# A two-sequence encoder layer on one core: part of the long sequence's products made by pairs with seven half products

## The chip, the cores and the metric

The kernel runs on one core of a Trainium2 chip. The metric is the device time of one execution in microseconds; the time given for a kernel is the median of its runs. PE is TensorE, DVE VectorE, ACT ScalarE, POOL GpSimd, SP SyncE, which issues most DMAs. Each engine works through its own instructions in the order in which they were written, and waits where an input or a buffer isn't ready.

## The reference, cut to what matters

One layer is applied to two sequences, of 512 and of 1024 tokens, with the same weights. The width is 1024.

```
u = x * (1 + scale) + shift                              # scale, shift, gate from a small condition
proj = u @ w_in                                          # segments: aq, af_f, af_b, ai, ag, rq, rk, rv, rg
q_a = silu(aq) * 128 ** -0.5                             # 8 heads of 128
logf, k = log(lb + (1 - lb) * sigmoid(fl)), (1 - lb) * sigmoid(-fl)       # fl = af_f forward, af_b backward
o_a = hgrn2(q_a, k_f, logf_f, ai) + flip(hgrn2(flip(q_a), flip(k_b), flip(logf_b), flip(ai)))
y_a = rms_norm(o_a) * a_norm_w * silu(ag)
y_r = layer_norm(retention in both directions of rope(rq), rope(rk), rv) * silu(rg)
g_a, g_r = split(sigmoid(u @ w_mg + b_mg))               # 2 x 1024 gate columns
s = (g_a * (y_a @ w_pa) + g_r * (y_r @ w_pb)) @ w_out
out = layer_norm(ALPHA * x + (1 + gate) * s) * ln_g + ln_b
```

hgrn2 is a gated linear attention: `o_t = sum over s <= t of q_t . (product of f between s and t) k_s v_s`, each of 128 columns with a decay f of its own.

## The kernel before

**Products.** All float32 products are made of F32R parts: a value is its high part plus the rest, and a product is three passes (high by low, low by high, high by high). A weight piece of 1024 x 128 comes as a raw load of 512 KB, ScalarE copies its high part (line 94), VectorE subtracts (line 103); `Stream` keeps the pieces in order of use, with four split pieces and two raw ones in flight, and `tick` splits the next one. `gemm_f` (line 310) makes 128 output columns for 512 tokens: 24 matmuls over 512 columns. `gemm_t` (line 321) makes 256 output columns for 128 tokens: 24 matmuls over 256 columns. Both give control back every six matmuls.

**Sequences and units.** The short sequence (g = 0) comes first, then the long one (g = 1), of two blocks of 512 tokens. In the long one there are eight A units, one for each head, whose two lanes are its two blocks, then four R units (retention), then the gates, then `pblock` and `oblock` (products with w_pa, w_pb and w_out, layer norm in `finish`). The spilled u, y and gates go through DRAM (`yd`, `gd`).

**An A unit.** `pre_A` makes three products for each lane: q, the forward and the backward forget logits; `evac` (lines 353 to 359) takes them out of PSUM with sigmoids, and `init_lane` (lines 340 to 346: one addition, two scalings, two multiplications on VectorE) starts a lane. `mid_A` makes values and the output gate (lines 390 to 393). `stages_A` is the chain of stages: levels 0, 1, 2, 4, 8, 16 (line 430) and 32, 64 (line 459), each of which multiplies queries and keys at one distance, takes the result with a predicated copy (439), multiplies the lanes' tiles by decays (414, and POOL's 416), and copies the next keys KM (403, 404); then four pairs of state transposes (489, 492) and state products (505, with updates 512 and 514); then for each lane the output products (542), its norm (546 to 557) and transposes of y (566 to 572).

**Order.** `interleave` writes a filler's matmuls with the stages spread among them by weights: the filler of unit i's stages is `mid` of unit i and `pre` of unit i + 1. Before the first unit of the long sequence the filler is `pre` of that unit, and the stages in it are the rest of the short sequence's `finish`. The gates of the long sequence (two blocks of 16 pieces) begin beside the last R unit and go on after it; from the fifth piece of the second block on, `load_y` issues the loads of y for the output products.

## Time and profile before

| | |
|---|---|
| runs | 2135.49, 2138.08, 2138.51 us, median 2138.08 |
| the profiled execution | span 2135.2 us |
| PE busy | 2108.5 us (99%), granted clock 0.998 |
| PEld, DVE, ACT, POOL busy | 1892.8 (89%), 1122.3 (53%), 746.7 (35%), 437.7 us (20%) |
| chain that ended last | PE 95% |
| long sequence, 738.5 us to the end: first products | 738.5 to 771.2 |
| A units | 771.2 to 1360, one each 74.1 us |
| last gates, to the output products | 1748.9 to 1946.2 for 870 matmuls of 512 columns |

Busy time is the sum of an engine's instructions; the chain is followed back from the last instruction through what released each step. An engine that is busy all the time bounds the kernel as long as its own instructions stand in the chain; where the chain leaves it, it waited, or was just about to.

### The profile page before, as it was taken

The numbers are of one execution on the slowest core, as the hardware profiler recorded it, in microseconds if no ns is written. First come the engines' busy times: TensorE is split into PE (matmuls) and PEld (weight loads), VectorE is DVE, ScalarE is ACT, GpSimd is POOL, SyncE is SP. The second block draws the span as 40 slices with busy tenths as digits, with TensorE's granted clock in tenths as the row PEclk, the third lists the DMA queues.
The fourth block names the chain that finished last, engine by engine and source line by source line (L and its number), as shares of the span: only waits on it lengthen the run. The fifth ranks groups of instructions, "written<-read, shape, count | busy, mean of one in ns | idle before, by whom it ended". The sixth has DMA issues, their size and how long they took to land.

```text
span 2135.2 us, 45792 instructions
## 1 busy us (share of the span) xinstructions
PE 2108.5 (99%) x19331; PEld 1892.8 (89%) x19331; DVE 1122.3 (53%) x2242; ACT 746.7 (35%) x1570; POOL 437.7 (20%) x668
## 2 busy tenths in 40 slices
PE   7999999999999999999999999999999999999997
PEld 5898899998888988899889889999999888889887
DVE  4856764644334965554565457353543442245657
ACT  3644553223322534444444435212121233322221
POOL 3322233321000332121121214332322100000101
PEclk9999999999999999999999999999999999999999
DMA  9322323246776421111111211212212256577752
GB/s 285 111 84 85 92 85 106 70 129 187 226 243 201 140 80 61 41 50 61 41 61 41 70 31 61 65 41 65 85 40 85 84 163 211 185 234 225 242 184 80
DMA packets 340205, 247.29 MB, mean 116 GB/s; under 512 B 9564, under 2 KB 303680, under 8 KB 338976
## 3 DMA queue, kind: packets, MB, share of 16 engines
q1 hardware_dynamic: 332112, 229.75, 34.9%
q10 hardware_dynamic: 6944, 12.59, 1.5%
q8 instruction: 152, 2.49, 0.5%
q0 software_dynamic: 944, 2.02, 0.3%
q14 instruction: 53, 0.43, 0.1%
HBM read 199.23 MB, written 45.10 MB: 114 GB/s over the span
## 4 chain that ended last, share of the span: by engine, by line
PE 95%; DMA 1%; DVE 1%; POOL 1%; issue 1%; ACT 1%; SPq 0%; POOLq 0%; DVEq 0%; ACTq 0%
PE g L310 41%; PE g L321 38%; PE l L542 2%; PE l L430 2%; PE t L505 2%; PE l L459 1%; PE l L742 1%; PE l L740 1%; PE t L677 1%; PE g L1171 1%; PE t L489 1%; PE l L1171 1%; PE t L707 1%; PE l L725 1%; PE t L1031 1%
## 5 line engine op out<-in xcount | busy, mean ns | idle before, releaser
L321 PE MATMUL g<-wh,u 128*128 128x256 f32 x3840 | 736.2, 287 | 0.0
L310 PE MATMUL g<-u,w 128*128 128x512 f32 x2736 | 671.7, 397 | 0.0
L321 PEld LDWEIGHTS g<-wh,u 128*128 128x128 f32 x3840 | 609.5, 191 | 8.9 <-issue 4.0
L310 PEld LDWEIGHTS g<-u,w 128*128 128x128 f32 x2736 | 499.7, 188 | 100.7 <-issue 1.2
L321 PE MATMUL g<-wl,u 128*128 128x256 f32 x1920 | 542.6, 283 | 0.0
L321 PEld LDWEIGHTS g<-wl,u 128*128 128x128 f32 x1920 | 367.1, 191 | 0.1
L103 DVE TENSOR_TENSOR w<-raw,w 128x1024 fp32r<-128x1024 f32 (+1 forms) x144 | 174.8, 1215 | 209.6 <-ACT w L94 209.5
L310 PE MATMUL g<-y,w 128*128 128x512 f32 x1152 | 261.8, 389 | 0.0
L310 PEld LDWEIGHTS g<-y,w 128*128 128x128 f32 x1152 | 216.1, 188 | 44.9
L414 DVE TENSOR_TENSOR X<-X,T 128x512 f32<-128x512 f32 x336 | 219.1, 698 | 22.2 <-issue 20.4
L94 ACT ACTIVATE w<-raw 128x1024 fp32r<-128x1024 f32 (+1 forms) x146 | 151.5, 1047 | 138.9 <-DMA raw<-in_w_pb 36.4
L103 DVE TENSOR_TENSOR wl<-raw,wh 128x1024 fp32r<-128x1024 f32 x98 | 122.6, 1262 | 104.2 <-ACT wh L94 104.2
L416 POOL TENSOR_TENSOR T<-T 128x512 f32<-128x512 f32 (+6 forms) x168 | 119.7, 739 | 83.6 <-DVE T L343 81.6
L94 ACT ACTIVATE wh<-raw 128x1024 fp32r<-128x1024 f32 x104 | 106.8, 1055 | 38.2 <-PE g L321 33.7
L321 PE MATMUL g<-wh,sl 128*128 128x256 f32 x384 | 109.0, 284 | 0.0
L446 POOL COPY A<-D 32x128 f32<-32x128 f32 x96 | 57.4, 598 | 248.4 <-DVE D L439 245.4
L321 PE MATMUL g<-wl,sh 128*128 128x256 f32 x384 | 107.6, 280 | 0.0
L321 PE MATMUL g<-wh,sh 128*128 128x256 f32 x384 | 107.6, 280 | 0.0
L403 ACT ACTIVATE KM<-X 128x256 f32<-128x256 f32 x120 | 51.5, 430 | 126.2 <-DVE X L414 122.5
L915 POOL TENSOR_SCALAR stat<-stat 128x1 f32<-128x1 f32 x12 | 9.2, 765 | 373.7 <-DVE stat L914 373.7
L826 ACT ACTIVATE sg<-g,vec 128x512 f32<-128x512 f32 x48 | 33.0, 687 | 127.2 <-PE g L310 127.2
L321 PEld LDWEIGHTS g<-wl,sh 128*128 128x128 f32 x384 | 73.3, 191 | 0.1
(197 smaller groups left out, 2390.7 us busy)
## 6 DMA issues: line engine op xcount, KB each, us to landing
raw<-in_w_in SPq DMA_DIRECT2D x122, 512.0 KB, 4.1
yd<-yT SPq DMA_DIRECT2D x96, 256.0 KB, 2.1
raw<-in_w_mg SPq DMA_DIRECT2D x48, 512.0 KB, 3.9
y<-yd SPq DMA_DIRECT2D x24, 1024.0 KB, 8.9
gd<-sg ACTq DMA_DIRECT2D x48, 256.0 KB, 2.7
raw<-in_w_pa SPq DMA_DIRECT2D x24, 512.0 KB, 4.7
raw<-in_w_pb SPq DMA_DIRECT2D x24, 512.0 KB, 4.0
gt<-gd SPq DMA_DIRECT2D x48, 256.0 KB, 4.7
```

Of the source, the lines that this page charges most:

```text
L94: self.nc.scalar.activation(out=hi, in_=raw, func=AF.Copy)
L103: self.lo.tensor_tensor(out=lo, in0=raw, in1=hi.bitcast(F32), op=ALU.subtract)
L310: T.matmul(ps, w[wi][:, k, :], a[ai](k), start=n == 0, stop=n == 3 * NK - 1)
L321: T.matmul(ps, a[ai](k, t0), w[wi][:, k, :], start=k == 0 and n == 0, stop=k == NK - 1 and ai == wi)
L403: S.activation(out=K4[:, :, 0, :], in_=halves(u.X[l][:, 0, :], h)[:, :, 0, :], func=AF.Copy)
L414: V.tensor_tensor(out=v, in0=v, in1=f, op=ALU.mult)
L416: G.tensor_tensor(out=T2, in0=Tv[:, :, :, 0], in1=Tv[:, :, :, 1], op=ALU.mult)
L430: T.matmul(ps[32 * i:32 * i + 32, c, :], km[:, c0:c0 + 32], qq, start=True, stop=True, tile_position=(0, 32 * i))
L446: G.tensor_copy(out=A[32 * i:32 * i + 32, :, 32 * i:32 * i + 32], in_=u.Dt[l][32 * i:32 * i + 32, :, :])
L505: T.matmul(ps[:, m, :], kt[:, m, :], u.Vt[l][:, c, :], start=True, stop=True)
L542: T.matmul(ps[:, c, :], a, b, start=i == 0, stop=i == len(mm) - 1)
L1171: T.matmul(acc[l, seg], w[wi][:, n0:n0 + 128], uh[0, 0, ai][:, k, :], start=k == 0 and n == 0, stop=k == 7 and n == 2)
```

## The change

For the long sequence, the twelve pairs of pieces in `PAIRED` (gate pieces 4 to 11, and the q and the forward forget pieces of all eight heads) are made ahead of the units. A pair is two pieces of 128 columns by two blocks of 512 tokens by 1024 of depth, seen as a 2 x 2 by 2 x 2 product of halves, and made with seven half products (line 939, 12 matmuls each) and sums, in place of eight (Winograd's form). The sums of the tokens' halves (`build_comb`, lines 903 to 915) are made once, those of the weights for each pair on GpSimd (`combine`, lines 926 to 929), the sums of the products on VectorE (lines 956 to 977). While the tokens' sums are made, gate pieces 0 to 3 run for both blocks (`FIRST`); gate pieces 12 to 15 stay at the end (`LAST`). Gates go to `gd` as before, finished q to `qd` and forget logits to `fd`, and `fetch` brings them back for each unit, so that `pre_A` of the long sequence makes only the backward product. The pool of the working tiles is closed and opened again around the pairs. The short sequence's last `finish` is written ahead of the early gates in one piece, and `load_y` begins at the first of the last four pieces. The other hunks (the pools' functions, the buffers' counts `C`: 8, `tt`: 2, `e`: 8, the releases of the pairs' raw pieces, removed comments) are left out here. Lines before and after: 310 is 358, 321 is 369, 430 is 500, 489 is 559, 505 is 575, 514 is 584, 542 is 612, 566 is 636, 340 to 346 are 388 to 394, 928 is 1114, 94 is 104.

```diff
         if j == len(self.todo) or (not self.parts and not self.open(j)):
             return False
         kind, ps = self.todo[j]
-        i = len(ps) - len(self.parts)
+        i = max(len(ps), 1) - len(self.parts)
         hi, lo = self.parts.pop(0)
-        raw = self.raws[j, i]
+        if kind in COMBINED:
+            m = COMBINED.index(kind)
+            if m == 0:
+                self.pairs[j] = self.combine(self.raws[j, 0], self.raws[j, 1])
+            raw = self.pairs[j - m][m]
+            if m == 2:
+                hi, lo = hi[:, 0:4], lo[:, 0:4]
+        else:
+            raw = self.raws[j, i]
         if kind == "k":
             raw = raw.rearrange("p k n -> p (k n)")[:, 0:768]
         self.nc.scalar.activation(out=hi, in_=raw, func=AF.Copy)
...
         [mk_unit("A", 1, i) for i in range(8)] + [mk_unit("R", 1, i) for i in range(4)],
     ]
+    EARLY = (0,1)
+    FIRST, LAST = range(4), range(12, 16)
+    PAIRED = [(None, n) for n in range(4, 12, 2)] + [(seg, h) for seg in EARLY for h in range(0, 8, 2)]
+    def order_pair(src, c0):
+        ws.add("s0", (src, c0), (src, c0 + 128))
+        for kind in COMBINED[1:]:
+            ws.add(kind)
     def order_pre(u):
         if u.kind == "A":
             for ls in u.wl:
                 h = u.lanes[ls[0]][0]
                 for seg in range(3):
-                    ws.add("f", (w_in, 1024 * seg + 128 * h))
+                    if u.g == 0 or seg not in EARLY:
+                        ws.add("f", (w_in, 1024 * seg + 128 * h))
         else:
             for ls in u.wl:
                 r = u.lanes[ls[0]][0]
...
     def pre_A(u):
         g = u.g
         prep_A(u)
+        if g:
+            fetch(u)
         for ls in u.wl:
-            for seg in range(3):
+            for seg in [seg for seg in range(3) if g == 0 or seg not in EARLY]:
                 j, w = ws.get()
                 for l in ls:
                     ps = gbank([128, 512])
                     yield from gemm_f(ps, w, u_f(g, u.lanes[l][1]))
                     evac(u, l, seg, ps)
                 ws.done(j)
+    def fetch(u):
+        for l in range(2):
+            h, b = u.lanes[l]
+            if 0 in EARLY:
+                u.X[l] = sb("X", [128, 4, 512])
+                u.q[l] = sb("q", [128, 512])
+                nc.sync.dma_start(u.q[l], qd[h, b])
+            for seg in (1, 2):
+                if seg in EARLY:
+                    ip, im = ((2, 0), (1, 3))[seg - 1]
+                    nc.sync.dma_start(u.X[l][:, ip, :], fd[seg - 1, h, b])
+        for l in range(2):
+            for seg in (1, 2):
+                if seg in EARLY:
+                    ip, im = ((2, 0), (1, 3))[seg - 1]
+                    X = u.X[l]
+                    S.activation(out=X[:, im, :], in_=X[:, ip, :], func=AF.Sigmoid, scale=-1.0)
+                    S.activation(out=X[:, ip, :], in_=X[:, ip, :], func=AF.Sigmoid)
     def mid_A(u):
         for wi, ls in enumerate(u.wl):
...
     ws.direct = gate_mm
-    def gates(g):
-        for b in range(NT[g] // 512):
-            for n in range(16):
+    def gate_evac(g, n, b, ps, t):
+        S.activation(out=t, in_=ps, func=AF.Sigmoid, bias=vec[:, 48 + n:49 + n])
+        S.dma_start(gd[g][n, :, 512 * b:512 * b + 512], t)
+    comb = {}
+    def build_comb():
+        for i in range(4):
+            comb[i] = [sb("C", [128, 4, 512], F32R, name="c") for _ in range(2)]
+        def piece(k):
+            f = {}
+            def sums():
+                for x, (b, half) in enumerate(((1, 0), (1, 1), (0, 0), (0, 1))):
+                    t = f[b, half] = sb("e", [128, 512], name="f")
+                    hi, lo = [uh[1, b, p][:, 4 * half + k, :].bitcast(F32) for p in range(2)]
+                    (V, G)[x % 2].tensor_tensor(out=t, in0=hi, in1=lo, op=ALU.add)
+            def mixes():
+                a21, a22, a11, a12 = f[1, 0], f[1, 1], f[0, 0], f[0, 1]
+                V.tensor_tensor(out=a22, in0=a21, in1=a22, op=ALU.add)
+                G.tensor_tensor(out=a21, in0=a11, in1=a21, op=ALU.subtract)
+                V.tensor_tensor(out=a11, in0=a22, in1=a11, op=ALU.subtract)
+                V.tensor_tensor(out=a12, in0=a12, in1=a11, op=ALU.subtract)
+            def parts():
+                for i, t in enumerate((f[1, 1], f[0, 0], f[1, 0], f[0, 1])):
+                    S.activation(out=comb[i][0][:, k, :], in_=t, func=AF.Copy)
+                    (V, G)[i % 2].tensor_tensor(out=comb[i][1][:, k, :], in0=t,
+                                                in1=comb[i][0][:, k, :].bitcast(F32), op=ALU.subtract)
+            return [Stage(sums), Stage(mixes), Stage(parts)]
+        return [s_ for k in range(4) for s_ in piece(k)]
+    def combine(r0, r1):
+        t12 = sb("tt", [128, 8, 128], name="t12")
+        t34 = sb("tt", [128, 8, 128], name="t34")
+        b11, b21, b12, b22 = r0[:, 0:4], r0[:, 4:8], r1[:, 0:4], r1[:, 4:8]
+        G.tensor_tensor(out=t12[:, 0:4], in0=b12, in1=b11, op=ALU.subtract)
+        G.tensor_tensor(out=t12[:, 4:8], in0=b22, in1=t12[:, 0:4], op=ALU.subtract)
+        G.tensor_tensor(out=t34[:, 0:4], in0=b22, in1=b12, op=ALU.subtract)
+        G.tensor_tensor(out=t34[:, 4:8], in0=b21, in1=t12[:, 4:8], op=ALU.subtract)
+        return r0, t12, r1[:, 4:8], t34
+    ws.combine = combine
+    def half(ps, w, k0, a, first, last):
+        n = 0
+        for k in range(4):
+            for wi, ai in ((0, 1), (1, 0), (0, 0)):
+                T.matmul(ps, w[wi][:, k0 + k, :], a[ai][:, k, :], start=first and n == 0, stop=n == 11,
+                         skip_group_check=True)
+                n += 1
+                if n % 6 == 0:
+                    yield 6 * 0.218
+    def gemm_pair(done):
+        a11, a12, a22 = [[uh[1, b, p][:, 4 * x:4 * x + 4, :] for p in range(2)] for b, x in ((0, 0), (0, 1), (1, 1))]
+        s1, s2, s3, s4 = [comb[i] for i in range(4)]
+        j0, w0 = ws.get()
+        p1 = gbank([128, 512])
+        yield from half(p1, w0, 0, a11, True, False)
+        j1, w1 = ws.get()
+        p6 = gbank([128, 512])
+        yield from half(p6, w1, 4, s2, True, True)
+        u2 = sb("e", [128, 512], name="u2")
+        S.activation(out=u2, in_=p1, func=AF.Copy)
+        yield from half(p1, w0, 4, a12, False, True)
+        ws.done(j0)
+        V.tensor_tensor(out=u2, in0=p6, in1=u2, op=ALU.add)
+        done(0, 0, p1)
+        p5 = gbank([128, 512])
+        yield from half(p5, w1, 0, s1, True, False)
+        ws.done(j1)
+        u4 = sb("e", [128, 512], name="u4")
+        V.tensor_tensor(out=u4, in0=p5, in1=u2, op=ALU.add)
+        (j2, w2), (j3, w3) = ws.get(), ws.get()
+        p7 = gbank([128, 512])
+        yield from half(p7, w3, 0, s3, True, False)
+        V.tensor_tensor(out=u4, in0=p7, in1=u4, op=ALU.add)
+        yield from half(p5, w2, 0, s4, False, True)
+        ws.done(j2)
+        c12 = sb("e", [128, 512], name="c12")
+        V.tensor_tensor(out=c12, in0=p5, in1=u2, op=ALU.add)
+        done(1, 1, u4)
+        yield from half(p7, w3, 4, a22, False, True)
+        ws.done(j3)
+        V.tensor_tensor(out=u2, in0=p7, in1=u2, op=ALU.add)
+        done(0, 1, c12)
+        done(1, 0, u2)
+    def pair_products():
+        for seg, x in PAIRED:
+            def done(b, i, what):
+                t = what if i + b else sb("e", [128, 512], name="c11")
+                if seg is None:
+                    gate_evac(1, x + i, b, what, t)
+                elif seg == 0:
+                    sg = sb("sg", [128, 512])
+                    S.activation(out=sg, in_=what, func=AF.Sigmoid)
+                    V.scalar_tensor_tensor(out=t, in0=what, scalar=qsc[:, x + i:x + i + 1], in1=sg, op0=ALU.mult,
+                                           op1=ALU.mult)
+                    S.dma_start(qd[x + i, b], t)
+                else:
+                    if i + b == 0:
+                        S.activation(out=t, in_=what, func=AF.Copy)
+                    S.dma_start(fd[seg - 1, x + i, b], t)
+            yield from gemm_pair(done)
+    def gates(g, ns=range(16), both=False):
+        nb = NT[g] // 512
+        for bs in [range(nb)] if both else [(b,) for b in range(nb)]:
+            for n in ns:
                 j, w = ws.get()
-                if b == NT[g] // 512 - 1:
-                    if n == 4:
+                if not both and bs[0] == nb - 1:
+                    if n == ns[4 if g == 0 else 0]:
                         more_y = load_y(g, 0, 0)
-                    if n >= 4 and more_y:
+                    if n >= ns[4 if g == 0 else 0] and more_y:
                         more_y.pop(0)()
-                ps = gbank([128, 512])
-                yield from gemm_f(ps, w, u_f(g, b))
-                t = sb("sg", [128, 512])
-                S.activation(out=t, in_=ps, func=AF.Sigmoid, bias=vec[:, 48 + n:49 + n])
-                S.dma_start(gd[g][n, :, 512 * b:512 * b + 512], t)
+                for b in bs:
+                    ps = gbank([128, 512])
+                    yield from gemm_f(ps, w, u_f(g, b))
+                    gate_evac(g, n, b, ps, sb("e" if both else "sg", [128, 512], name="sg"))
                 ws.done(j)
                 if rows_g:
                     gate_out(*rows_g.pop(0))
...
             yield from g_
     LEAD_IN = 2.5
-    PRE = {"A": 31.1, "R": 20.9}
+    PRE = {("A", 0): 31.1, ("R", 0): 20.9, ("A", 1): 31.1 * (3 - len(EARLY)) / 3, ("R", 1): 20.9}
     MID = {"A": 20.9, "R": 41.9}
     def run(gen):
-        for _ in gen:
-            pass
+        interleave(gen, 1.0, [], marks, ws)
+    def run_stages(stages):
+        while stages:
+            stages.pop(0).fn()
     with tc.manual_schedule():
         startup()
...
         for g in range(2):
             us = groups[g]
             if g:
-                interleave(pre(us[0]), 12.0, more, marks, ws)
+                close_pool()
+                open_pool("st")
+                interleave(gates(1, FIRST, True), 41.9, build_comb(), marks, ws)
+                interleave(pair_products(), 1.0, [], marks, ws)
+                close_pool()
+                open_pool("at1")
+                run(pre(us[0]))
             for i, u in enumerate(us):
                 st = stages_A(u) if u.kind == "A" else stages_R(u)
                 if i + 1 < len(us):
                     nx = us[i + 1]
-                    interleave(chain(mid(u), pre(nx)), MID[u.kind] + PRE[nx.kind], st, marks, ws, LEAD_IN)
+                    interleave(chain(mid(u), pre(nx)), MID[u.kind] + PRE[nx.kind, g], st, marks, ws, LEAD_IN)
                 else:
-                    interleave(chain(mid(u), gates(g)), MID[u.kind] + 60.0, st, marks, ws)
+                    fill = gates(g, LAST) if g else gates(g)
+                    interleave(chain(mid(u), fill), MID[u.kind] + (41.9 if g else 60.0), st, marks, ws)
             more = []
             nb = NT[g] // 512
             for b in range(nb):
...
                 interleave(oblock(g, b, st, g == 1 and b == nb - 1), 42.0, stages, marks, ws)
                 ws.lo = nc.vector
                 more = st["finish"]
+                if g == 0:
+                    run_stages(more)
+        close_pool()
 # ---- launch: one core; inputs and outputs as the reference has them ----
```

PE, A units: from level 2's matmuls to level 4's (line 500, both lanes), with the filler of `mid` between them; before, 24 such matmuls and more stand between two levels.

```order
L500 MATMUL l<-X,KM 32x32 x15
L369 MATMUL g<-wh,u 128x256
L369 MATMUL g<-wl,u 128x256
L369 MATMUL g<-wh,u 128x256 x2
L369 MATMUL g<-wl,u 128x256
L369 MATMUL g<-wh,u 128x256 x2
L369 MATMUL g<-wl,u 128x256
L369 MATMUL g<-wh,u 128x256 x2
L369 MATMUL g<-wl,u 128x256
L369 MATMUL g<-wh,u 128x256
L500 MATMUL l<-X,KM 32x32 [waits PE_49,Activation_49]
```

Between these two levels there are 12 matmuls over 256 columns. In the changed order 12 also stand ahead of level 1, level 16 and the first state transposes, and 24 ahead of levels 2, 8, 32 and 64.

PE, end of an A unit before: the last output product, the transposes of y of both lanes, and the next unit's products.

```order
L542 MATMUL l<-S,X 128x128
L310 MATMUL g<-u,w 128x512 x12
L566 MATMUL t<-ident,y 128x128 [waits Activation_49] x4
L310 MATMUL g<-u,w 128x512 x6
L566 MATMUL t<-ident,y 128x128 [waits Activation_49] x4
```

And after, at the same place.

```order
L612 MATMUL l<-S,X 128x128
L636 MATMUL t<-ident,y 128x128 [waits Activation_49] x4
L358 MATMUL g<-u,w 128x512 x6
L636 MATMUL t<-ident,y 128x128 [waits Activation_49] x4
L369 MATMUL g<-wh,u 128x256
```

The first lane's transposes now follow the second lane's output product at once, and six product matmuls stand ahead of the second lane's.

DVE, the same part of an A unit before: the last state updates (line 514), the two lanes' outputs by their gates (548), and the next unit's `init_lane` of lane 0 (340 to 346).

```order
L514 SCALAR_TENSOR_TENSOR S<-S,T_11181,t 128x128
L514 SCALAR_TENSOR_TENSOR S<-S,T_11166,t 128x128
L548 TENSOR_TENSOR y<-l,G 128x512
L340 TENSOR_TENSOR KM<-X 128x512
L343 TENSOR_SCALAR T_11368<-X,oml,lbm 128x512 x2
L346 TENSOR_TENSOR X<-T_11368,q 128x512 x2
L548 TENSOR_TENSOR y<-l,G 128x512
```

And after.

```order
L388 TENSOR_TENSOR KM<-X 128x512
L391 TENSOR_SCALAR T_11140<-X,oml,lbm 128x512 x2
L394 TENSOR_TENSOR X<-T_11140,q 128x512 x2
L584 SCALAR_TENSOR_TENSOR S<-S,T_11016,t 128x128
L584 SCALAR_TENSOR_TENSOR S<-S,T_11001,t 128x128
L113 TENSOR_TENSOR w<-raw,w 128x1024
L618 TENSOR_TENSOR y<-l,G 128x512 x2
```

`init_lane` of lane 0 moved from behind the first lane's output to ahead of the last state updates.

## Rows read from the trace of the kernel before

**Rows 1.** The page: busy times and the chain by engine.

```profile
PE 2108.5 (99%) x19331; PEld 1892.8 (89%) x19331; DVE 1122.3 (53%) x2242; ACT 746.7 (35%) x1570; POOL 437.7 (20%) x668
...
PE 95%; DMA 1%; DVE 1%; POOL 1%; issue 1%; ACT 1%; SPq 0%; POOLq 0%; DVEq 0%; ACTq 0%
```

**Rows 2.** The chain, 700 to 860 and 1700 to 1960 us: start, length, what.

```profile
738.50 32.66 PE g L310 x144
...
1748.94 197.22 PE g L310 x870
```

**Rows 3.** Stretches: length, busy PE, PEld, DVE, ACT, POOL, PEclk, DMA share, GB/s.

```profile
845.26:919.36 74.10, 74.10 (x913) 65.91 (x912) 40.85 (x78) 32.68 (x87) 15.61 (x26) 1.00 0.17 51
...
1289.90:1360.00 70.10, 69.88 (x1005) 67.87 (x1004) 40.50 (x83) 30.25 (x81) 25.11 (x37) 1.00 0.18 58
```

**Rows 4.** The chain of one A unit, 985 to 1067.5 us.

```profile
1014.90 0.69 PE l L430 x50
1015.59 3.06 PE g L321 x24
...
1054.40 0.44 PE t L505 x4
1054.84 1.38 PE g L310 x6
1056.22 2.45 PE l L542 x22
```

**Rows 5.** Timeline of a level, 1003 to 1010 us: start, length, engine, line, operation.

```profile
1005.76 0.89 PE L430 MATMUL l<-X,KM 128*32 128x32 f32 x64
1006.46 0.30 DVE L439 COPY_PREDICATED D<-mask,l 128x128 f32<-128x128 uint8 x1 [5.52 <-PE l L430]
...
1007.99 0.44 ACT L404 ACTIVATE KM<-X 128x256 f32<-128x256 f32 x1
...
1009.39 0.44 ACT L404 ACTIVATE KM<-X 128x256 f32<-128x256 f32 x1
```

**Rows 6.** The chain of the last A unit, 1289 to 1325 us.

```profile
1311.89 0.42 ACT KM L404
```

**Rows 7.** Timeline of VectorE, 1033 to 1065 us.

```profile
1054.88 0.61 DVE L514 SCALAR_TENSOR_TENSOR S<-S,T,t 128x128 f32<-128x128 f32 x2 [0.94 <-PE t L505]
...
1060.90 0.69 DVE L340 TENSOR_TENSOR KM<-X 128x512 f32<-128x512 f32 x1 [0.28 <-ACT X L359]
...
1062.42 1.29 DVE L346 TENSOR_TENSOR X<-T,q 128x512 f32<-128x512 f32 x2
```

**Rows 8.** The chain after the last output product, 1325 to 1362 us.

```profile
1350.44 1.43 PE g L321 x12
...
1353.73 0.94 PE t L566 x4
```

**Rows 9.** Timeline of GpSimd, then ScalarE, 742 to 760 us.

```profile
744.20 0.79 POOL L915 TENSOR_SCALAR stat<-stat 128x1 f32<-128x1 f32 x1 [11.50 <-DVE stat L914]
...
746.83 1.29 POOL L929 TENSOR_TENSOR h<-h,lb 128x512 f32<-128x512 f32 x1 [0.84 <-ACT h L928]
748.28 0.79 POOL L915 TENSOR_SCALAR stat<-stat 128x1 f32<-128x1 f32 x1 [0.15 <-DVE stat L914]
...
746.03 0.73 ACT L928 ACTIVATE h<-h,stat 128x512 f32<-128x512 f32 x1 [5.11 <-POOL stat L916]
...
754.98 1.05 ACT L94 ACTIVATE wh<-raw 128x1024 fp32r<-128x1024 f32 x1
```

**Rows 10.** Timeline of VectorE, 742 to 760 us: two like pairs of passes.

```profile
744.15 1.41 DVE L919 SCALAR_TENSOR_TENSOR h<-h,stat,lg 128x512 f32<-128x512 f32 x2
...
751.08 2.34 DVE L919 SCALAR_TENSOR_TENSOR h<-h,stat,lg 128x512 f32<-128x512 f32 x2
```

**Rows 11.** The page: loads of y.

```profile
y<-yd SPq DMA_DIRECT2D x24, 1024.0 KB, 8.9
```

**Rows 12.** The page: low parts on VectorE, busy us and mean ns.

```profile
L103 DVE TENSOR_TENSOR w<-raw,w 128x1024 fp32r<-128x1024 f32 (+1 forms) x144 | 174.8, 1215 | 209.6 <-ACT w L94 209.5
```

More of the change, by code (lines that the diff above doesn't have):

```diff
@@ L103, in flush @@
         self.lo.tensor_tensor(out=lo, in0=raw, in1=hi.bitcast(F32), op=ALU.subtract)
-        del self.raws[j, i]
+        kind = self.todo[j][0]
+        if kind in COMBINED:
+            m = COMBINED.index(kind)
+            if m == 0:
+                del self.raws[j, 0]
+            elif m == 2:
+                del self.raws[j - 2, 1]
+            elif m == 3:
+                del self.pairs[j - 3]
+            self.parts = []
+        else:
+            del self.raws[j, i]
         if not self.parts:
@@ L284, in layer @@
         else:
+            for n in FIRST:
+                ws.add("f", (w_mg, 128 * n))
+            for seg, x in PAIRED:
+                order_pair(*((w_mg, 128 * x) if seg is None else (w_in, 1024 * seg + 128 * x)))
             order_pre(us[0])
@@ L290, in layer @@
         for b in range(NT[g] // 512):
-            for n in range(16):
+            for n in LAST if g else range(16):
                 ws.add("f", (w_mg, 128 * n))
```

19 lines of the change are left out of this document (15 added, 4 removed).

## The prediction, made before the changed kernel was run

> **What bounds the kernel now.** I read the busy table first: PE is busy 2108.5 us of the 2135.2 us span and 95% of the chain that ended last lies on it, so nearly every matmul counts in full, and nothing else does until it makes PE wait [rows 1]. The per-line chain tells what a matmul costs: 870 of them over 512 columns, back to back, take 197.22 us, 0.2267 us each [rows 2]. The table by stretches then gives a pattern: the eight A units of the long sequence follow each other every 74.1 us (one of the cycles is shown), PE is busy all of it at a granted clock of 1.00, VectorE 40.8, ScalarE 32.7, GpSimd 15.6 [rows 3]. So an A unit has idle room on the other engines, but its stages form one long dependent chain, which is hidden only because PE has other products to do between two stages. The remaining views (chain and timeline inside one unit) are for the question how much of such filler each stage needs.
>
> **Part 1, the matmuls.** In the order before, 3888 matmuls run over 512 columns, after it 3744 (2736 plain and 1008 half products). 144 fewer at 0.2267 us is **-32.6 us**. That is twelve pairs times twelve matmuls: 84 in place of 96. Nothing else leaves PE. By place: the products ahead of the units lose 96 (-21.8 us), each of seven unit-to-unit cycles loses 96 (-21.8 each), the gates at the end lose 576 (-130.6), the four early gate pieces add 192 (+43.5), the pairs add 1008 (+228.5).
>
> **Part 2, the A-unit cycle with less filler.** A cycle without waits would be 74.09 - 21.76 = 52.3 us. But the chain of stages is as long as before, and the same stages now share 96 fewer filler matmuls: where a level followed its predecessor over 36, 24 or 18 pieces of filler, it now does so over 12 or 24 of 256 columns. What a level needs can be read in one place of before [rows 5]: its matmuls start at 1005.76; the predicated copy of lane 0 starts at 1006.46, its multiplications follow, ScalarE finishes that lane's new keys at 1008.43 (1007.99 + 0.44), 2.67 after the level's start; lane 1's keys follow 1.40 later, at 1009.83, 4.07 after the start. A level takes PE 0.69 and 24 filler matmuls 3.06 [rows 4], together 3.75: lane 0 finds its keys, lane 1 (which starts 0.35 later) just about finds them. This is the edge, and before shows it: in the last A unit, whose filler is 24 at every level, the chain leaves PE at a level and runs through VectorE and ScalarE's key copies [rows 6]. With 12 matmuls (half of 3.06, so 1.53) the next level is due at 2.22: lane 0 waits 0.45, and lane 1's half another 1.05, 1.5 in all at most; it is less when VectorE, which can start on lane 0 during the wait, is ahead for the following level. The changed order has 12 matmuls ahead of levels 1, 4 and 16 and of the first state transposes, 24 ahead of the others. Level 1's keys don't hang on a predicated copy; I cost it at nothing. I take 0.95 us for level 4, 1.3 for 16, 0.6 for the first transposes (0 to 1.5 each) and 0.3 for level 2, which stands over 24 but after the longer first level (0 to 0.5). What hides the remaining levels is the 24 matmuls; without them each would cost up to 1.5.
>
> Two more waits are in the second half of the unit. The **last state update**: before, it ran right after its matmuls (from 1054.88, 0.61 us) and the first output product started on time at 1056.22 [rows 4, 7]. In the changed order the next unit's start of lane 0 (one addition, two scalings, two multiplications: from 1060.90 to 1063.71, 2.81 us) stands ahead of it on VectorE, because its inputs come by DMA and no product has to be waited for. Between the third and the last state product PE has 6 matmuls (1.38 us) and the product itself (0.44); VectorE begins the 2.81 us some 0.6 after the third, so ends 3.4 after it, the update of 0.6 ends at 4.0, and PE would be there at 1.38 + 0.44 + 1.38 = 3.2. With the hand-overs I take 1.1 us (0 to 2.8). The **output transposes**: the second lane's transposes need squares on ScalarE, a power on GpSimd and a scaling on ScalarE; where before has only 12 pieces of 256 columns ahead of each lane's, they end 4.24 us after the last output product (1350.44 to 1354.68) [rows 8]. The changed order leaves 0.44 + 1.38 + 0.44 = 2.26 of work in that time: a wait of 1.98; I take 1.85 (1 to 2.2). Together 6.1 us a cycle, bounds 3 and 8.5: 58.4 instead of 74.1. Over seven cycles **+42.7 us** (21 to 60), more than all that the missing matmuls save.
>
> What stands behind a waiting PE is everything, since it works in order. The fetched logits (two 256 KB loads a lane) are issued about a unit ahead, and four sigmoids on ScalarE replace the four that read PSUM: nothing.
>
> **Part 3, start of the long sequence.** The rest of the short sequence's layer norm used to be spread under the first unit's products; now it stands in one piece ahead of the early gates on every engine. From before: GpSimd begins at 744.20; one round takes 4.08 us (744.20 to 748.28), because GpSimd's last addition of one row block comes ahead of the next block's first step [rows 9]. GpSimd's first step waits for VectorE, which has one low part of 1.22 [rows 12] ahead of it there; without that I put the start at 742.8, and four rounds' ScalarE steps end at 742.8 + 3 x 4.08 + 2.56 = 757.6. Behind them stand two weight splits (1.05 each) and only then the first gate's sigmoid (about 0.6), which frees a PSUM bank at about 760.3. PE, having three banks, has done three products at 738.5 + 3 x 5.44 = 754.8. **+5.4 us** (0 to 7).
>
> **Part 4, pairs.** A pair lasts 84 x 0.2267 = 19.0 us on PE. VectorE has in it three and a half low parts (1.22 each) and up to eight passes of 0.7, about 10; ScalarE three and a half high parts and some four copies or sigmoids, about 6; GpSimd four subtractions at 1.29 [rows 9], about 5. All fit. The tightest hand-over is the copy of the first half product out of its bank, behind a DMA issue on ScalarE; it has about half a microsecond. I take **+1 us** for the twelve (0 to 10). Rows that bear on the upper end: VectorE's pair of passes over two SBUF inputs takes 1.41 us alone and 2.34 when it meets GpSimd's addition [rows 10].
> The Trainium skill, "SBUF — State Buffer", section "Who interferes with whom", says that a VectorE instruction with two SBUF inputs and a GpSimd instruction that reads SBUF exclude each other, each for the other's whole length. The 2.34 agrees with that. By the rule every subtraction of the weight mixing can push a VectorE pass back by its length; that would be the third rival below.
>
> **Part 5, the tail.** The first loads of y for the output products (1 MB in four pieces) are issued during the last four gates instead of the fifth on. The last piece is issued about 5.4 us before the gates end, a pair of such loads needs 8.9 us to land [rows 11], and the first product reaches it about 2.7 us in: +0.8 without other traffic; I take **+1.5** (0 to 5).
>
> **Sum.** -32.6 + 42.7 + 5.4 + 1 + 1.5 = +18.0 on the profiled 2135.2. The median of the runs, 2138.08, lies 2.9 above that span; so 2138.1 + 18 = **2156 us**.
>
> **Rivals.** (a) *The cover holds.* VectorE gets ahead during each wait, so that the levels cost little, and the last state update slips ahead; 2.5 us a cycle, 17.5 in all, and 3 for the start: 2138.1 - 32.6 + 17.5 + 3 = 2126. For it: PE is idle only 0.2 us in the last A unit although its chain passes through VectorE and ScalarE [rows 3, 6]. Against: that unit has twice the filler at levels 4 and 16. With all waits hidden it would be 2105.5. (b) *A draw.* With the 7.9 us of parts 3 to 5, 3.5 us a cycle give 2138; 2.9 to 4.1 us a cycle are within 0.2%, which is about what a measurement here can tell from no change. (c) *VectorE held up by GpSimd in the pairs*, the other way up: one subtraction of 1.29 meeting the pass that frees a bank, every pair, costs 0.8 beyond its half microsecond of margin, on up to two places: 10 to 20 us more, 2166 to 2176. It decides once the bank's copy is more than 0.5 late. Against: the mixing is issued a piece ahead, mostly off that path. (d) *It does less than it says*, excluded for the count: the changed order has 3744 matmuls.
>
> **Chances.** The forecast (4.2 to 8 us a cycle, 2143 to 2170) 0.57, (c) or cycles longer still 0.13, (b) 0.13, (a) 0.17. The forecast's own range is 2143 to 2170. The range to hold 8 in 10 takes in the draw and half of (a) below and (c) above: 2124 to 2178. Slower by over 0.2% (over 2142.4): 0.70; within: 0.13; faster (under 2133.8): 0.17.
>
> **What would show it.** In the profile after: A units at a pitch of 58 to 59 us (52.3 if the cover holds, over 60 if it is worse); the chain leaving PE at levels 4 and 16 for the predicated copy, the multiplications and the key copies; VectorE's additions of the next unit's lane 0 between the last two state updates and PE idle ahead of the output product; 1.8 us ahead of the second transposes, released by ScalarE; PE idle about 5 us near the fourth early gate, released by ScalarE's sigmoid; pairs at 19 to 19.2 us. A pitch of 55 us or less would make the forecast wrong, as would pairs above 20.

## The result, and the profile after

The changed kernel takes 2176.22 us (median of four runs, 2175.91 to 2177.3) against 2137.3 for the kernel before on the same chips: 1.0184 times as long, 95% interval 1.017 to 1.0199, slower by some 39 us. The forecast was 2156: the sign was right, the size half of what came. 2176.22 lies above the forecast's own range (2143 to 2170) and inside the wide one (2124 to 2178). The profiled execution spans 2175.5 us, 40.3 more than before's 2135.2.

The page of the kernel after, against [rows 1]: busy times, and the chain by engine.

```profile
PE 2100.0 (97%) x19187; PEld 1879.1 (86%) x19187; DVE 1212.7 (56%) x2342; ACT 774.8 (36%) x1614; POOL 550.8 (25%) x736
...
PE 48%; DVE 6%; POOL 4%; issue 4%; ACT 3%; DMA 0%; ACTq 0%; DVEq 0%; POOLq 0%; SPq 0%
```

144 matmuls are gone, as counted, but PE's busy time fell by only 8.4 us in place of 32.6: some matmuls became slower, and some waits inside a row of the trace count as busy. PE's share of the chain that ended last fell from 95% to 48%. The waits of PE (in total, times, longest, us):

```profile
PE l L500 <- ACT KM L474: 14.3, 23, 0.9
PE t L636 <- ACT y L627: 8.3, 7, 1.2
PE g L939 <- POOL c L915: 7.7, 1, 7.7
PE l L612 <- DVE S L584: 7.1, 7, 1.0
PE g L358 <- ACT sg L885: 6.2, 2, 4.6
...
PE t L559 <- DVE X L484: 3.2, 7, 0.5
PE g L939 <- ACT sg L885: 2.9, 1, 2.9
...
PE g L939 <- ACT u L956: 0.7, 4, 0.2
```

Four of them are the A units' (lines 500, 559, 612, 636): three come seven times, once in each cycle, and the one at line 500 comes 23 times, some three a cycle. Three belong to the start of the long sequence: the gate's sigmoid (885) that frees a bank, and the token sums (915). Busy time in two stretches of the kernel after, from the first early gate to the end of the pairs and one A-unit cycle, to be read against [rows 3]:

```profile
core 0: us, PE busy (x) PEld busy (x) DVE busy (x) ACT busy (x) POOL busy (x), PEclk, DMA share, GB/s
739.12:1035.89 296.77, 279.16 (x1203) 227.88 (x1201) 160.96 (x182) 96.55 (x129) 113.78 (x80) 0.97 0.31 104
1106.22:1164.88 58.66, 53.93 (x817) 48.59 (x816) 37.17 (x73) 29.66 (x84) 16.36 (x26) 1.00 0.20 65
```

The first stretch holds 1200 matmuls over 512 columns, 272.0 us at 0.2267: it lost 24.7 us. The cycle is 58.66 long, where 52.33 would do: it lost 6.33, seven times. With landmarks in both traces (start of the long sequence, end of the first unit's own products, end of the eighth unit, start of the output products, end) the 40.3 us split up as 0.6 + 24.9 + 45.4 + 0.4 + 1.7 of losses, less 32.6 of matmuls. The 45.4 are the seven cycles (44.3) and 1.1 in the eighth unit.

PE's timeline in that cycle shows at which levels it waits (the rows at 1118.88, 1122.04 and 1129.42 are the second lane's halves of levels 2, 4 and 16), and the second lane's transposes, which also stretch:

```profile
1118.88 0.46 PE L500 MATMUL l<-X,KM 128*32 128x32 f32 x32 [0.31 <-ACT KM L474]
...
1122.04 0.46 PE L500 MATMUL l<-X,KM 128*32 128x32 f32 x32 [0.68 <-ACT KM L474]
...
1129.42 0.46 PE L500 MATMUL l<-X,KM 128*32 128x32 f32 x32 [0.94 <-ACT KM L474]
...
1163.68 1.21 PE L636 MATMUL t<-ident,y 128*128 128x128 f32 x4 [1.18 <-ACT y L627]
```

In the chain before, the same four transposes take 0.44 us:

```profile
1065.29 0.44 PE t L566 x4
```

Where the 24.9 went, in PE's timeline after (start, length, matmuls, and in brackets the idle time before):

```profile
739.12 16.51 PE L358 MATMUL g<-u,w 128*128 128x512 f32 x72
760.23 24.04 PE L358 MATMUL g<-u,w 128*128 128x512 f32 x96 [4.60 <-ACT sg L885]
785.89 5.78 PE L358 MATMUL g<-u,w 128*128 128x512 f32 x24 [1.62 <-ACT sg L885]
791.50 2.88 PE L939 MATMUL g<-u,w 128*128 128x512 f32 x12
797.31 3.09 PE L939 MATMUL g<-c,w 128*128 128x512 f32 x9 [2.93 <-ACT sg L885]
808.11 1.65 PE L939 MATMUL g<-c,w 128*128 128x512 f32 x3 [7.71 <-POOL c L915]
809.55 4.16 PE L939 MATMUL g<-u,w 128*128 128x512 f32 x12
813.55 8.32 PE L939 MATMUL g<-c,w 128*128 128x512 f32 x36
```

The 4.60 is the wait that was forecast. The other three, 12.3 us, are the token sums: the 2.93 and the 1.62 name ScalarE, but the sigmoid there stood behind ScalarE's copies of the sums. And the rows at and after the waits are long. The 9 matmuls at 797.31 take 3.09 us (2.0 at 0.2267), and the 96 gate matmuls 24.04 (21.8 at 0.2267, and about 0.16 for the last one's modelled end). The stretches say why:

```profile
760.20:785.90 25.70, 24.05 (x97) 19.41 (x97) 19.12 (x16) 9.15 (x14) 19.41 (x13) 0.92 0.34 109
797.30:808.10 10.80, 3.09 (x9) 1.97 (x9) 9.39 (x9) 3.79 (x6) 8.10 (x7) 0.56 0.30 97
830.00:860.00 30.00, 30.00 (x134) 24.85 (x133) 11.97 (x15) 10.71 (x14) 9.66 (x8) 1.00 0.31 102
```

Cut more finely, around the first and the last two waits:

```profile
757.70:764.40 6.70, 4.17 (x10) 3.30 (x11) 5.75 (x5) 3.17 (x5) 5.16 (x3) 0.50 0.62 216
764.50:798.50 34.00, 29.45 (x128) 23.72 (x128) 25.97 (x23) 13.35 (x21) 26.57 (x17) 1.00 0.21 71
798.70:812.20 13.50, 5.79 (x15) 4.02 (x14) 11.31 (x10) 3.73 (x6) 10.72 (x8) 0.50 0.19 59
```

The granted clock (third number from the right) is 0.92 and 0.56 in the longer stretches because it was at the lower of its two levels (0.50, that is 1.2 GHz) for a part of each, and at 1.00 otherwise. From these rows the lower clock cost about 5 us: 2.1 on the 96, 0.9 on the 9, and 2.0 on the next 15, which took 5.4 us (808.11 to 813.55) in place of 3.4. The Trainium skill, "TensorE: Matmul & The Clock Gate", section "HAM oscillation — how this bites in real kernels", says that waits between bursts of matmuls bring the clock down and that the next burst starts slow; these rows agree. The waits (16.9), the lower clock (5) and the waits for the copies in the pairs (0.7) make 22.6 of the 24.7; the rest is spread over the rows in small parts.

What held the sums up stands on VectorE and GpSimd after (VectorE's rows first, then GpSimd's of the same stretch):

```profile
760.06 3.44 DVE L903 TENSOR_TENSOR f<-u 128x512 f32<-128x512 f32 x2
...
764.55 0.68 DVE L907 TENSOR_TENSOR f<-f 128x512 f32<-128x512 f32 x1
766.65 0.69 DVE L909 TENSOR_TENSOR f<-f 128x512 f32<-128x512 f32 x1 [1.41 <-POOL f L908]
...
779.69 1.76 DVE L907 TENSOR_TENSOR f<-f 128x512 f32<-128x512 f32 x1 [3.69 <-POOL f L903]
```

```profile
759.01 3.93 POOL L903 TENSOR_TENSOR f<-u 128x512 f32<-128x512 f32 x2
765.31 1.30 POOL L908 TENSOR_TENSOR f<-f 128x512 f32<-128x512 f32 x1 [2.37 <-DVE f L907]
768.35 1.47 POOL L926 TENSOR_TENSOR t<-raw 128x512 f32<-128x512 f32 x1 [1.74 <-DMA raw<-in_w_mg]
```

Alone, such a pass takes VectorE 0.69 and GpSimd 1.30; side by side 1.72 and 1.97. The split has a second price: VectorE waits for GpSimd's part of each round, 1.41 us in the first, and 3.69 more in the second, because GpSimd had the first pair's weights to mix (from 768.35) before its part. Four such rounds, begun only after the layer norm (757.8), end at 809.7.

### The profile page after: what moved, and what is told of

Read it like the earlier page. It is cut to its first block, busy times and chain, and to the rows that moved or that the text cites. A ratio compares the mean times of both kernels' runs of the same rounds, so it can differ in the third digit from the quotient of the medians.

```text
span 2175.5 us, 45946 instructions
## 1 busy us (share of the span) xinstructions
PE 2100.0 (97%) x19187; PEld 1879.1 (86%) x19187; DVE 1212.7 (56%) x2342; ACT 774.8 (36%) x1614; POOL 550.8 (25%) x736
## 4 chain that ended last, share of the span: by engine, by line
PE 48%; DVE 6%; POOL 4%; issue 4%; ACT 3%; DMA 0%; ACTq 0%; DVEq 0%; POOLq 0%; SPq 0%
PE g L369 20%; PE g L358 12%; PE g L939 9%; DVE X L484 3%; POOL A L516 1%; PE t L575 1%; POOL T L486 1%; ACT sg L616 1%; PE t L747 1%; PE l L500 1%; PE l L812 1%; PE l L810 1%; POOL D L621 1%; PE t L559 1%; ACT y L627 1%
## 5 line engine op out<-in xcount | busy, mean ns | idle before, releaser
L358 PE MATMUL g<-u,w 128*128 128x512 f32 x1584 | 399.5, 400 | 6.2 <-ACT sg L885 6.2
L358 PEld LDWEIGHTS g<-u,w 128*128 128x128 f32 x1584 | 288.8, 189 | 64.7 <-ACT sg L885 7.1
L113 DVE TENSOR_TENSOR w<-raw,w 128x1024 fp32r<-128x1024 f32 (+2 forms) x132 | 156.3, 1185 | 154.0 <-ACT w L104 153.8
L104 ACT ACTIVATE w<-raw 128x1024 fp32r<-128x1024 f32 (+2 forms) x134 | 133.6, 1007 | 162.3 <-DMA raw<-in_w_pb 36.8
L486 POOL TENSOR_TENSOR T<-T 128x512 f32<-128x512 f32 (+6 forms) x168 | 133.2, 820 | 116.8 <-DVE T L391 114.8
L939 PE MATMUL g<-c,w 128*128 128x512 f32 x576 | 136.3, 392 | 10.6 <-POOL c L915 7.7
L939 PEld LDWEIGHTS g<-c,w 128*128 128x128 f32 x576 | 108.7, 189 | 34.3 <-POOL c L915 8.4
L939 PE MATMUL g<-u,w 128*128 128x512 f32 x432 | 103.8, 394 | 0.7 <-ACT u L956 0.7
L939 PEld LDWEIGHTS g<-u,w 128*128 128x128 f32 x432 | 81.9, 190 | 19.6 <-ACT u L956 2.4
L516 POOL COPY A<-D 32x128 f32<-32x128 f32 x96 | 51.6, 538 | 170.2 <-DVE D L509 167.2
```

What stands on the lines that cost most here:

```text
L104: self.nc.scalar.activation(out=hi, in_=raw, func=AF.Copy)
L113: self.lo.tensor_tensor(out=lo, in0=raw, in1=hi.bitcast(F32), op=ALU.subtract)
L358: T.matmul(ps, w[wi][:, k, :], a[ai](k), start=n == 0, stop=n == 3 * NK - 1)
L486: G.tensor_tensor(out=T2, in0=Tv[:, :, :, 0], in1=Tv[:, :, :, 1], op=ALU.mult)
L516: G.tensor_copy(out=A[32 * i:32 * i + 32, :, 32 * i:32 * i + 32], in_=u.Dt[l][32 * i:32 * i + 32, :, :])
L939: T.matmul(ps, w[wi][:, k0 + k, :], a[ai][:, k, :], start=first and n == 0, stop=n == 11, skip_group_check=True)
```

## The experiments

Each was timed beside the kernel before on the same chip. The first three are about the start of the long sequence, the others about the units, the pairs, or both.

**e1_comb_dve.** All token sums on VectorE.

```diff
-                    (V, G)[x % 2].tensor_tensor(out=t, in0=hi, in1=lo, op=ALU.add)
+                    V.tensor_tensor(out=t, in0=hi, in1=lo, op=ALU.add)
...
-                G.tensor_tensor(out=a21, in0=a11, in1=a21, op=ALU.subtract)
+                V.tensor_tensor(out=a21, in0=a11, in1=a21, op=ALU.subtract)
...
-                    (V, G)[i % 2].tensor_tensor(out=comb[i][1][:, k, :], in0=t,
+                    V.tensor_tensor(out=comb[i][1][:, k, :], in0=t,
```

> The changed kernel with all of the token sums (build_comb) on VectorE, none on GpSimd; the rest as it is. Theory 1 (in the changed kernel VectorE and GpSimd hold each other up: VectorE's two-input passes take 1.7 us beside GpSimd's and 0.69 alone): 12 passes of 0.69 a round, four rounds, are 33 us, with six low parts of 1.2 about 41 us from 757.7, so the sums end at about 799 in place of 809.7; from the start of the early gates to the end of the first unit's own products the loss falls from 24.9 to about 17, time about 2168. Rival 2 (it is the amount of work on VectorE, and GpSimd takes part of it off): the sums end later than 809.7, time 2176 to 2185. Rival 3 (only the layer norm ahead of them counts): no change in the waits, 2176.

Measured 2166.47 us, ratio 1.014 (1.0125 to 1.0155). The loss from the first early gate to the end of the pairs is 15.9. VectorE's timeline in this run:

```profile
757.28 2.48 DVE L903 TENSOR_TENSOR f<-u 128x512 f32<-128x512 f32 x4
...
769.36 4.67 DVE L903 TENSOR_TENSOR f<-u 128x512 f32<-128x512 f32 x4
...
794.62 3.56 DVE L915 TENSOR_TENSOR c<-f,c 128x512 fp32r<-128x512 f32 x4
798.10 1.21 DVE L113 TENSOR_TENSOR w<-t,w 128x1024 fp32r<-128x1024 f32 x1
```

Four sums take VectorE 2.48 us alone, where two of them took it 3.44 beside GpSimd. The same four take 4.67 from 769.36 on, where GpSimd mixes the first pair's weights until 772.29. One engine is done at 798.2, where the two together needed until 809.7. Theory 1 holds: the split is what slows the sums. How much of that is the longer passes and how much the waits of one engine for the other's part isn't told apart, since this edit takes both away. The Trainium skill, "SBUF — State Buffer", section "Who interferes with whom", has the two engines exclude each other in such passes. The pattern agrees; 1.72 in place of 0.69 is 1.03 more, not quite GpSimd's whole 1.30.

**e2_two_steps.** The layer norm under its own early gates, then the sums under four more.

```diff
-    FIRST, LAST = range(4), range(12, 16)
-    PAIRED = [(None, n) for n in range(4, 12, 2)] + ...
+    FIRST, SECOND, LAST = range(4), range(4, 8), range(12, 16)
+    PAIRED = [(None, n) for n in range(8, 12, 2)] + ...
...
+                interleave(gates(1, FIRST, True), 41.9, more, marks, ws)
                 close_pool()
                 open_pool("st")
-                interleave(gates(1, FIRST, True), 41.9, build_comb(), marks, ws)
+                interleave(gates(1, SECOND, True), 41.9, build_comb(), marks, ws)
...
-                if g == 0:
-                    run_stages(more)
```

> The changed kernel, with the short sequence's last layer norm spread again under early gate pieces 0 to 3, and the token sums under four further early gate pieces (4 to 7, taken out of the pairs: ten pairs in place of twelve, 24 matmuls or 5.4 us more). Theory 1 (the loss at the start comes from the layer norm in one piece, 5 to 15 us, and from sums that take 51 us where 46 are covered): no wait behind the layer norm, about 5 us behind the sums, loss at the start 24.9 down to about 7, time 2176 - 18 + 5.4 = 2163.5. Rival (the loss is in the pairs themselves, GpSimd's subtractions against VectorE): loss at the start stays above 18, time 2176 to 2181.

Measured 2163.65, ratio 1.0125 (1.0108 to 1.0142). PE runs 384 gate matmuls without a wait, in 87.23 us; one wait of 2.5 for the sums is left (with a stretch of 3.2 us at the lower clock right behind it), and the loss up to the end of the pairs is 6.3. Theory 1 holds.

**e3_no_sums.** The token sums left out.

```diff
-            comb[i] = [sb("C", [128, 4, 512], F32R, name="c") for _ in range(2)]
+            b, x = ((0, 0), (0, 1), (1, 0), (1, 1))[i]
+            comb[i] = [uh[1, b, p][:, 4 * x:4 * x + 4, :] for p in range(2)]
+        return []
```

> The changed kernel without the token sums: the pairs use the plain halves of u in their place (so q, the forward logits and half of the gates are other values), every matmul and all else as it is. Theory 1: what is left of the loss at the start is the wait behind the layer norm, about 5 us, and about 1 us of lower clock after it: 24.9 down to 6, time about 2157. Rival (the pairs are held up by GpSimd and VectorE): loss stays above 15, time above 2166.

Measured 2163.3, ratio 1.0123 (1.0108 to 1.0138). The time lies between the two, nearer to the rival's 2166 than to 2157. The trace, of an execution of 2160.98 us, speaks for theory 1: the wait behind the layer norm is there with 4.59, the others are gone, and the loss is 9.6, nearer to 6 than to 15. The stretch after that wait shows what I had put too low:

```profile
757.10:787.00 29.90, 29.90 (x121) 24.53 (x122) 4.19 (x4) 6.78 (x9) 8.66 (x6) 0.91 0.43 137
...
757.10:762.30 5.20, 5.20 (x12) 4.13 (x13) 1.04 (x1) 1.28 (x2) 0.00 (x0) 0.50 0.80 245
762.40:787.00 24.60, 24.60 (x110) 20.38 (x109) 3.14 (x3) 5.40 (x8) 8.66 (x6) 1.00 0.35 114
```

Its 120 matmuls take 29.9 us where 27.2 would do, because the first 5.2 us ran at a granted clock of 0.50: one wait of 4.6 costs 2.7 more behind it. The pairs lost about 2 in all.

**e4_early_q.** Only q and the gates in pairs, by `EARLY = (0,)`.

> The changed kernel with only q and the gates in pairs (EARLY = (0,)): the forward forget logits are made in the units again, so each A-unit cycle has 48 matmuls over 512 columns (10.9 us) more filler, and four pairs fewer are made (48 matmuls more in all, 10.9 us). Theory 1 (the 6.3 us that a cycle loses is lack of filler): about 1.5 us a cycle is left, time 2176 - 7 x 4.8 + 10.9 = 2153. Rival (the cycle loses because the fetched lane starts early on VectorE, and by the order of stages): the loss stays near 6 us a cycle, time about 2187.

Measured 2149.94, ratio 1.0063 (1.0048 to 1.0078). The cycle is 64.4 us, 1.2 over the 63.2 that its work takes. Theory 1 holds by its number: with twelve pairs the kernel is 26 us slower than with eight. The edit changes the order too, though: lane 0's start now has to wait for a product and stands behind the last state updates on VectorE again (1098.56 in this run, the last update at 1097.89), so the 1.0 us a cycle of that wait goes by order and not by filler. The waits at the levels fall from 14.3 to 2.4 us in all, and those ahead of both kinds of transposes are gone.

**e5_init_late.** The next unit's lane 0 started with lane 1.

```diff
-            if seg == 2:
-                init_lane(u, l)
+            if seg == 2 and (u.g == 0 or l == 1):
+                for i in range(2) if u.g else (l,):
+                    init_lane(u, i)
```

> The changed kernel, with the next unit's lane 0 started on VectorE together with lane 1 (after the unit's last output), in place of ahead of the last state updates. Theory 1 (PE waits 1.0 us a cycle at the first output product because those 2.8 us stand ahead of the last state updates): that wait goes, seven times 1.0, pitch 58.66 to about 57.7, time about 2169. Rival (the chain through the unit is what counts, and the wait moves on to the next level 0, which now finds both lanes late): pitch unchanged, time 2175 to 2178.

Measured 2185.62, ratio 1.0232 (1.0218 to 1.0246), 9.4 us slower than the changed kernel, more than the rival allowed. PE's waits in it:

```profile
PE l L501 <- ACT KM L475: 15.5, 26, 1.0
PE l L501 <- DVE KM L388: 8.8, 7, 2.1
...
PE l L501 <- DVE X L394: 7.3, 6, 1.2
```

The wait for the last state update (7.1) is gone, and 16.1 us of waits for the two lanes' starts came in its place. Theory 1 falls, and the rival's mechanism holds: the wait moved on to the next level 0, and grew. With so little filler neither place tried for the 2.8 us a lane was off the path.

**e6_q_spread.** Seven pairs (q, six gate pieces), the layer norm under pieces 0 and 1, the sums on VectorE under pieces 2 to 5.

```diff
-    EARLY = (0,1)
-    FIRST, LAST = range(4), range(12, 16)
+    EARLY = (0,)
+    FIRST, SECOND, LAST = range(2), range(2, 6), range(12, 16)
...
-    PAIRED = [(None, n) for n in range(4, 12, 2)] + ...
+    PAIRED = [(None, n) for n in range(6, 12, 2)] + ...
...
+                interleave(gates(1, FIRST, True), 20.9, more, marks, ws)
                 close_pool()
                 open_pool("st")
-                interleave(gates(1, FIRST, True), 41.9, build_comb(), marks, ws)
+                interleave(gates(1, SECOND, True), 41.9, build_comb(), marks, ws)
...
```

The sums' edit is that of e1, the removal of the layer norm in one piece that of e2.

> What the runs so far point to: pairs for q and six gate pieces only (seven pairs, 84 matmuls fewer than before, -19.0 us); the short sequence's last layer norm under early gate pieces 0 and 1, the token sums under pieces 2 to 5 and all on VectorE. Theory 1: cycles lose 1.2 us each (8.4), the start 2 to 3, the end 2: 2136.5 - 19.0 + 13 = about 2130, faster than before by 0.3%. Rival (a loss of 15 us at the start stays, whatever the order): 2143, slower than before.

Measured 2130.26 against 2136.51, ratio 0.9972 (0.9961 to 0.9983): faster than both kernels. The early gates (288 matmuls) and one A-unit cycle:

```profile
737.70:803.01 65.31, 65.31 (x290) 54.06 (x289) 53.44 (x78) 23.93 (x35) 18.38 (x17) 1.00 0.38 125
1088.34:1152.73 64.39, 64.10 (x864) 57.16 (x864) 38.59 (x74) 30.81 (x85) 19.02 (x26) 1.00 0.19 59
```

PE is busy throughout the first at a clock of 1.00: the early gates cost nothing any more, and the seven pairs behind them lose 1.5 us. The cycle is 64.39 long, again 1.2 over its work. Theory 1 holds.

**e7_q_spread_late.** As e6, the second lane's transposes of y carried over into the next unit's stages.

```diff
-                st = stages_A(u) if u.kind == "A" else stages_R(u)
+                st = late + (stages_A(u) if u.kind == "A" else stages_R(u))
+                late = [st.pop()] if g and u.kind == "A" else []
```

> As e6_q_spread, and the transposes of y of a unit's second lane are written a little after the next unit's first products, in place of at the unit's end, so that the norm ahead of them has time. Theory 1 (half of the 1.2 us that a cycle still loses is PE stretched over these transposes, 1.01 in place of 0.44): 0.6 us less a cycle, 4 us in all, about 2126. Rival (the next unit's levels come later by as much, or are squeezed): as e6_q_spread or slower by up to 5 us.

Measured 2143.84, ratio 1.003 (1.0018 to 1.0041): 13.6 slower than e6, more than the rival allowed. The wait for the last state update came back (7.2 in seven times), and 5.5 ahead of the state transposes. The carried stage moved the others: lane 0's start stands ahead of the last state update on VectorE again (1145.78, the update at 1148.50 in one cycle), as in the changed kernel. Theory 1 falls.

**e8_gates_only.** As e6 with `EARLY = ()`: three pairs, the units as before.

> As e6_q_spread, with pairs for six gate pieces only (three pairs, 36 matmuls fewer than before, -8.2 us): the units keep all three of their own products, the cycle its filler. Theory 1: cycle pitch 74.1 as before, the loss at the start and the end 4 to 5 us, time 2133. Rival (units lose as much without their fetched q, for another reason): pitch above 75, time above 2140.

Measured 2130.5, ratio 0.9976 (0.9967 to 0.9986); PE's waits for keys in the units are 0.5 us together, as before. Theory 1 holds for the units, and the rest lost 2 in place of 4 to 5.

**e9_plain_ahead.** As e6, its seven pairs made by plain products ahead of the units.

```diff
...
-            yield from gemm_pair(done)
+            for i in range(2):
+                j, w = ws.get()
+                for b in range(2):
+                    ps = gbank([128, 512])
+                    yield from gemm_f(ps, w, u_f(1, b))
+                    done(b, i, ps)
+                ws.done(j)
...
```

The token sums are left out too.

> As e6_q_spread, with the same seven pairs of pieces made ahead and spilled, but by plain products: eight half products' worth of matmuls, no token sums, no mixed weights. Theory 1 (a pair saves PE its twelve matmuls, 2.7 us, and almost nothing of it is lost inside the pairs): 84 matmuls or 19.0 us more than e6_q_spread, less the 0.6 us that the pairs wait: 2148 to 2150. Rival (the pairs give their saving back in their own waits and PE rows): 2130 to 2140.

Measured 2147.74, ratio 1.0051 (1.0038 to 1.0063): 17.5 us over e6 by the medians and 18.8 by the profiled spans (2147.0 and 2128.2), where 84 matmuls are 19.0. A pair gives 2.5 to 2.7 of its 2.7 us; the intervals are too wide (each some 2.5 us to either side) to tell these apart. Theory 1 holds: the pairs are sound, the loss lies around them.

**e10_late_transposes.** As e6 with a weight of 2.8 in place of 1.5 for the second lane's transposes.

> As e6_q_spread, with the weight of the second lane's transposes of y raised from 1.5 to 2.8, which puts 12 matmuls over 512 columns ahead of them in place of 6, and takes 6 to 12 from level 4 (36 to 24 of 256 columns) and the first state transposes. Theory 1 (PE is stretched 0.57 us a cycle over these transposes and has slack elsewhere): seven times 0.57 less, up to 0.3 a cycle back at the levels: 2126.5 to 2130. Rival (the level chain has no slack left at 24): 2130 to 2135.

Measured 2132.92, ratio 0.9984 (0.9975 to 0.9993). The time alone, 2.7 us over e6 with intervals that overlap, would not decide. The traces do: the stretch over the second lane's transposes is gone as hoped (0.60 in place of 1.18), but PE's waits for keys rose from 2.6 to 5.2 and those ahead of the state transposes from none to 3.9. The rival holds: at 24 matmuls a level has no slack.

**e11_start_only.** The changed kernel with e6's start: eleven pairs, q and logits fetched.

> The changed kernel with only its start mended as in e6_q_spread (layer norm under early gate pieces 0 and 1, token sums on VectorE under pieces 2 to 5; eleven pairs in all, -29.9 us of matmuls against before); q and the forward logits fetched, so the A-unit cycles stay as in the changed kernel. Theory 1 (two separate losses: 45 us in the cycles, 25 at the start, of which this takes all but 2): 2136.3 - 29.9 + 45.4 + 2 + 2 = 2156, pitch 58.66. Rival (the cycles were slow as a consequence of the start, by the clock or by late spills): pitch 55 or less, time 2130 to 2140.

Measured 2157.32, ratio 1.01 (1.0082 to 1.0118). The cycle is 58.67, and the units' waits are those of the changed kernel to 0.1 us, but for one more of 0.8. From the first early gate to the end of the pairs the loss is 2.0. Theory 1 holds: the two losses are separate. Mending the start gave 18.9 us, although one pair fewer cost 2.7.

## Why the prediction was right in its direction and wrong in its size

- **Matmuls, -32.6.** Right: the count is right, and e9 shows that a pair's saving arrives, as nearly as the runs can tell.
- **A-unit cycles, +42.7.** Right: 44.3 in the seven cycles, and 1.1 in the eighth unit. The pitch was to be 58 to 59 and is 58.66. By waits: levels 2.04 a cycle (2.55 forecast), state transposes 0.46 (0.6), last state update 1.02 (1.1), second transposes 1.19 and 0.77 of stretch, 1.21 in place of 0.44, together 1.96 (1.85). At the levels the cycle shown has 0.31, 0.68 and 0.94 at 2, 4 and 16, where 0.3, 0.95 and 1.3 were forecast. These make 5.5 of the 6.33; a listed wait begins only at the modelled end of the matmul before it, 0.1 to 0.3 us late each time. For the cause: with 48 more filler matmuls (and the old order of lane 0's start) 1.2 is left in e4, and in e10 the same total, with some of it taken from a level, doubles the waits for keys (2.6 to 5.2).
- **Start of the long sequence, +5.4, and pairs, +1.** This is the step that failed: 24.7 in place of 6.4, which is 18 of the 22 us that the forecast missed on the span. Part 3 named the layer norm in one piece and its wait (5.4 forecast, 4.60 measured; the end of the layer norm, forecast at 757.6, came at 757.7), but costed nothing else that stands in that place. The 48 passes of the token sums, begun behind that layer norm, were not in the sum at all; part 4 added up VectorE's and GpSimd's work for a pair only. They made 12.3 us of waits. And about 5 us came from the lower clock after the waits, of which I had no term. The runs show it from several sides: without the sums only the layer norm's wait and its lower clock stay (e3), with the layer norm spread and four more gate pieces beside the sums one wait of 2.5 us for the sums stays (e2), and with both mended PE waits for neither (e6, e11) and 1.5 to 2 us are left, in the pairs.
- **Rival (c)** had the right mechanism, VectorE and GpSimd holding each other up, in the wrong place: in the pairs PE waits 0.7 us for the copy that I thought tight. In the sums e1 shows it: one engine alone is faster than both. That its 2166 to 2176 ends where the time came out is luck, and so is it that the wide range, which (c) had stretched, takes the time in: the pairs, where (c) put 10 to 20 us, lost about 2.
- **Tail, +1.5.** 0.4 up to the output products, no wait there, and 1.7 later. 1.4 of it are the products with w_out, 46.07 and 31.69 us after, 45.23 and 31.11 before, without a wait in the trace. They take 46.07 and 31.69 in e1 to e11 too, whichever pieces are paired and also without pairs (e9); why is open.
- **Rival (b)**, that 3.5 us a cycle would make a draw, can't be tested as such; but e6, e8 and e10 show what it takes. The only versions that are faster than before are those that cover the start and leave the units half of the filler that the change took (e6, e10) or all of it (e8); e7, with as much but in another order, is not. They gain 6 us of the 19.0 that the pairs save in e6, 3 of the same 19.0 in e10, and 6 of 8.2 in e8. e6 gives the rest back in the cycles (some 8), the pairs (1.5) and the tail (about 2).

## What to carry to other kernels

Where PE is busy 99% of the time, its matmuls are also the cover of the other engines' chains: before taking some out of a stretch, read how long each stage's chain is there, and what would cover it. A step that prepares something ahead needs its own sum of work on each engine, from the moment the engine is free, not from where it is written. And an elementwise step that is split between VectorE and GpSimd may take longer than on VectorE alone.

## What the runs showed of the hardware that I had not expected

VectorE's pass over two 128x512 inputs in SBUF took 0.69 us alone and 1.72 beside GpSimd's like pass, and GpSimd's 1.30 became 1.97; together they were slower than VectorE with all of it (2.48 for four). PE's wait of 4.6 us in e3 was followed by 5.2 us at a granted clock of 0.50, which cost 2.7 us more; after the wait of 7.7 us in the changed kernel the next 15 matmuls took 5.4 us in place of 3.4. Shorter waits were followed by the lower clock too: after one of 2.46 us in e2 the clock was 0.50 from 833.2 to 836.4, and after one of 2.19 us in e4 from 786.1 to 789.4.
